# A convolution's sums in a PSUM bank and tile each, its chains in pairs, and another place for sigmoids, scans and gate products

## The chip, the core and the metric

The kernel runs on one core of a Trainium2 chip. The metric is the device time of one execution in microseconds; lower is better. TensorE (PE) multiplies matrices into PSUM, VectorE (DVE) and GpSimd (POOL) work element by element, ScalarE (ACT) does functions such as sigmoid and the casts, SyncE (SP) issues the DMAs. A tile is a piece of on-chip memory with up to 128 partitions; an f32 tile of 128x512 in PSUM is one bank.

## The reference, cut to what matters

One even layer (a Conformer convolution branch and a bidirectional RG-LRU branch beside each other) and one odd layer (a pooling mixer) over 1024 latent tokens and 256 context tokens with 1024 channels. The change lies in the even layer:

```python
z = h @ p["w_in"]
va, vg, ga, xb, gb = split(z)                       # 1024 channels each
u = va * sigmoid(vg)                                # the linear unit
u = depthwise_conv(u, conv_w, conv_b, (15, 15))     # 31 taps along the tokens
y_a = silu(layernorm(u)) * silu(ga)
u2 = depthwise_conv(xb, sconv_w, sconv_b, (2, 1))   # 4 taps, context and latent
r, i = sigmoid(u2 @ w_r + b_r), sigmoid(u2 @ w_i + b_i)    # per head and direction
a = exp(-8 * r * softplus(-lam))
bx = sqrt(1 - a * a) * (i * u2)
h_t = a_t * h_{t-1} + bx_t                          # forwards and backwards
y_b = (h_forward + h_backward) * silu(gb)
out = concatenate([y_a, y_b]) @ w_out
```

## The kernel before

All data lie with channels on the partitions and tokens along the row, so that a channel tile (128 channels) of the 1024 latent tokens is a 128x1024 tile. Each f32 product is made of three matmuls in fp32r: the weights and the activations are split into a high part (a cast on ACT, names `wh_` and `h0h`) and a low part (a subtraction, `wl_` on POOL and `h0l`), and PE adds high x high, high x low and low x high. A product of 128x512 over the 8 tiles of input channels takes 24 matmuls.

The even layer's input projection is a loop over j, the 8 channel tiles (= heads of the LRU). An iteration does, on PE: vg of j (two halves of 512 tokens), va of j, xbc (the context part of xb of j+1, 256 tokens), then the gates of j (12 steps: two directions, two gates, three pieces of tokens) with the product xb of j+1 between them. The other engines follow:
- DVE: the short convolution `uc` of j (a first tap on ACT, three others on DVE: `first_tap`, `other_taps`), `ul` (low part of uc), `u` = va times the sigmoid, the scans of the iteration before (`rec_scan` for each direction: one SCALAR_TENSOR_TENSOR and a scan over the context and one over the latent tokens), their sum (`rec_sum`), and steps of the 31-tap convolution wherever `fill(n)` stands.
- ACT: the cast `uh` of uc, tanh, exp and sqrt of the recurrence of the iteration before (`rec_tanh`, `rec_exp`, `rec_root`), the sigmoids `sg` of vg, those of the gates (named `l`, straight out of PSUM), and casts of weights. A change of the function table costs an ACT_TABLE_LOAD.
- POOL: low parts of weights, `rec_input` (gate times uc) and `rec_scaled` (the same times the root), for each direction.

The 31-tap convolution of a channel tile is a generator, `conv` (L500). It sums even and odd tokens apart: one 128x512 sum `acc_` of the even tokens, one, `late`, of the odd ones, then, after it has added odd and even tokens into `uo`, a second chain of taps with added pairs of weights `wsum`. `fill(n)` takes n steps from the convolution begun first of those whose `u` is whole. The two sums are the two halves of one two-bank tile from `wide` (L91). What stays open when the loop ends is done in pairs of tiles (L910 to L912), outside the written order.

Behind the loop, the products gb of j = 0 to 7 (PE), their silu `sb` (ACT), `yr` = yb_raw times sb (DVE; the sum of the scans comes back from DRAM), its split `ybh`, `ybl`, with conv steps between. Then come the products wob (output projection of y_b), the mean `mu` over `lnsum` (the sum of the finished convolutions, two matmuls on PE), the LayerNorm of u (subtraction, squares, root), and the products ga.

The order of all this is written by hand. The helper `on` (L433, its instruction is issued at L437, which is why the profile shows L437 for nearly all of it) makes an instruction issue behind the last one that `on` gave to the same engine. DMAs go out on SP in the order in which `raw_load` (L463) and the others are called; `raw_split` (L468) casts and subtracts. Where a tile's pool has no free buffer, the instruction that takes one waits for the last reader of the oldest: raw weights `wr`, `wh` and `wl` have 2 buffers each, `t` tiles (sg, sb, split gate weights) 4, one-bank PSUM tiles 4, and of `wide` there is one buffer for each of two tags, `cv` (conv) and `xb`. The six tiles `l` hold gates and roots and are passed on from one iteration to the next.

Of the kernel before, what the change touches and what calls it, by code (L numbers as in the profile page):

```python
# [9 lines left out]
F32 = mybir.dt.float32  # L10
# [45 lines left out]
def body(ctx, tc, xT, ctxT, cc, ccol, modT, modW, win, gw, wout, wu, grp, wg, wo1, small, edge, ident, outT):  # L56
# [34 lines left out]
    def wide(name, n):  # L91
        return pc.tile([P, S], F32, tag=("cv", "xb")[n % 2], name=name)
# [85 lines left out]
    def rstd(acc, eps, name, wn=0):  # L178
        n = acc.shape[-1]
        ps = psum(f"ms_{name}") if n < H else wide(f"ms_{name}", wn)  # L180
        nc.tensor.matmul(ps[:, :n], ones, acc, start=True, stop=True)
        rt = ttile(f"sq_{name}")
        nc.scalar.activation(rt[:, :n], ps[:, :n], AF.Sqrt, bias=eps)
        nc.vector.reciprocal(acc, rt[:, :n])


    def rstd_cols(acc, name, idD, rpool, wn):
        n = acc.shape[-1]
        nt = n // P
        ps = wide(f"ms_{name}", wn)  # L190
# [9 lines left out]
        nc.tensor.matmul(ps[:, H : H + n], ones, t, start=True, stop=True)  # L200
        return ps[:, H : H + n]
# [66 lines left out]
    with ExitStack() as sctx:  # L268
# [99 lines left out]
        for i, t in enumerate((cL, cC)):  # L368
            ps = wide(f"c_{i}", i)
            for h in range(2):  # L370
                nc.tensor.matmul(ps[:, HALF[h]], ones[:1], cx[i][:1, HALF[h]], start=True, stop=True)
            nc.scalar.activation(t, ps, AF.Silu, scale=float(D))
# [127 lines left out]
    def conv(j, n):  # L500
        acp = wide(f"conv{j}", n)
        ue, uo = us[j][:, 0::2], us[j][:, 1::2]
        acc_, late, bias = acp[:, HALF[0]], acp[:, HALF[1]], col(O_CONVB + j)
        w = lambda k: col(O_CONVW + 31 * j + k)
        vec(nc.vector.tensor_scalar, out=acc_, in0=ue, scalar1=w(15), scalar2=None, op0=mult)
# [3 lines left out]
        for n in range(NT + 1):  # L509
# [6 lines left out]
        vec(nc.vector.scalar_tensor_tensor, out=edge_junk, in0=uo[:, H - 8 :], scalar=1.0, in1=taps[:, j, 0:16:2],  # L516
            op0=mult, op1=mult, accum_out=edges[:, j : j + 1])
# [4 lines left out]
        vec(nc.vector.scalar_tensor_tensor, out=acc_, in0=uo, scalar=wsum[:, j, 7:8], in1=ue, op0=mult, op1=sub)  # L522
# [21 lines left out]
    def fill(n):  # L544
        while n > 0:
            try:
# [5 lines left out]
                going[0] = conv(begun[0], 0)  # L552
                begun[0] += 1

    with ExitStack() as actx:
# [79 lines left out]
        xb = wide("xb0", 1)  # L635
# [13 lines left out]
        for j in range(KT):  # L649
# [53 lines left out]
            if state is not None:  # L703
# [6 lines left out]
            xb = wide(name if final else f"xb{j + 1}", 1)  # L710
# [8 lines left out]
            for n, _ in enumerate(gate_steps(j, (gwh, gwl), (uh, ul), gates)):  # L719
# [12 lines left out]
        gps = {0: [xb[:, h] for h in HALF], 1: [psum(f"gb1_{h}") for h in range(2)]}  # L732
# [8 lines left out]
        all_of(mm3_fixed(gps[1][0], w, (hh, hl), HALF[0]))  # L741
# [834 lines left out]
```

## Time and profile before

| what | value |
|---|---|
| runs of the kernel, median of 3 | 1409.15 us (1409.05 to 1413.17) |
| the profiled execution, its own time | 1413.85 us |
| its span | 1412.0 us |
| busy PE / DVE / ACT / POOL | 92% / 86% / 44% / 25% |
| mean granted TensorE clock | 0.962 of full |
| loop over j and its end | 157 to 528 us of the span |
| gb, wob, to the mean of the LayerNorm | 528 to 674 us |
| ga and all behind it | from 718 us |

The profile is of one execution, that of 1413.85 us; times within it count from the start of its span. A row of the timeline has start, length, engine, line, operation, out<-in by the program's names without buffer numbers, matrix or tile sizes and, in brackets, the idle time before it and what ended it; x8 means that eight instructions in a row are shown as one. A row of the waits has the waiting instruction, the one that released it, the total in us, how often, and the longest. A busy share of 92% is a mean over stages with different limits, so the stages have to be looked at one by one.

### The profile page before, as it was taken

How to read it: one execution, taken by the hardware profiler on the slowest of the kernel's cores; microseconds unless marked ns; L12 is line 12 of the kernel's file. 1: busy time of each engine (PE TensorE's matmuls, PEld its weight loads, DVE VectorE, ACT ScalarE, POOL GpSimd, SP SyncE). 2: the span in 40 equal slices, each digit the busy share in tenths (PEclk: the TensorE clock that was granted, in tenths of full speed). 3: DMA queues.
4: the chain of work that ended last, by engine and by line, in shares of the span. 5: the costliest groups of instructions: out<-in, count | busy, mean ns of one | idle time of the engine just before them, and what ended most of it. 6: DMA issues, size and time to landing. Idle time of an engine off the chain costs nothing.

```text
span 1412.0 us, 15817 instructions
## 1 busy us (share of the span) xinstructions
PE 1295.2 (92%) x5664; PEld 1051.2 (74%) x5664; DVE 1215.2 (86%) x1790; ACT 628.3 (44%) x900; POOL 349.0 (25%) x172
## 2 busy tenths in 40 slices
PE   7888999899889839999869999999999999999896
PEld 4467888778777728878658788878878888778685
DVE  7985799999999999989688875899999986976775
ACT  6352745564556522210543534654334433544442
POOL 5182445454544524422402002200000000000002
PEclk9899999999999979999979999999999999999998
DMA  9744011111021212344135436523433334667633
GB/s 352 267 134 157 23 67 38 60 38 68 30 82 38 75 34 93 112 154 152 62 126 185 162 124 203 170 91 134 142 127 113 126 113 142 233 207 249 229 118 120
DMA packets 82866, 181.79 MB, mean 129 GB/s; under 512 B 7778, under 2 KB 27618, under 8 KB 82788
## 3 DMA queue, kind: packets, MB, share of 16 engines
q1 hardware_dynamic: 74340, 176.60, 36.3%
q10 hardware_dynamic: 8448, 4.20, 1.0%
q8 instruction: 44, 0.72, 0.2%
q14 instruction: 34, 0.28, 0.1%
HBM read 136.72 MB, written 44.04 MB: 128 GB/s over the span
## 4 chain that ended last, share of the span: by engine, by line
PE 39%; DVE 26%; DMA 8%; issue 3%; ACT 2%; POOL 2%; POOLq 0%; DVEq 0%; SPq 0%; ACTq 0%
DVE conv L437 7%; DVE l L437 6%; PE gb L437 4%; PE wob L128 2%; PE wob L126 2%; PE wob L127 2%; PE ga L126 2%; PE ga L127 2%; PE ga L128 2%; DVE u L437 2%; DVE uc L437 1%; DMA yr_t<-y_t 1%; DMA wr_wu<-wu 1%; PE qb_g L837 1%; PE qb_g L840 1%
## 5 line engine op out<-in xcount | busy, mean ns | idle before, releaser
L437 DVE SCALAR_TENSOR_TENSOR conv<-u,sm,conv 128x505 f32<-128x505 f32 (+6 forms) x196 | 147.1, 751 | 5.8
L1396 POOL TENSOR_TENSOR o<-x,rr 128x256 f32<-128x256 f32 (+1 forms) x9 | 8.1, 930 | 459.5 <-ACT rr L1384 456.8
L437 ACT ACTIVATE l<-g,sm 128x512 f32<-128x512 f32 (+1 forms) x96 | 58.8, 618 | 83.0 <-PE g L437 60.5
L96 POOL TENSOR_TENSOR wl_wu<-wr_wu,wh_wu 128x1024 fp32r<-128x1024 f32 x16 | 39.4, 2469 | 154.6 <-ACT wh_wu L95 149.5
L437 POOL TENSOR_TENSOR l<-l,uc 128x1280 f32<-128x1280 f32 x16 | 50.3, 3144 | 98.7 <-PE g L437 71.6
L437 PE MATMUL gb<-h0h,wh_gb 128*128 128x512 f32 x128 | 51.7, 404 | 23.0 <-ACT sb L437 23.0
L437 POOL TENSOR_TENSOR l<-l,l 128x1280 f32<-128x1280 f32 x16 | 54.1, 3383 | 72.2 <-ACT l L437 72.2
L437 DVE SCALAR_TENSOR_TENSOR conv<-u,wsum,conv 128x505 f32<-128x505 f32 (+6 forms) x92 | 69.0, 750 | 2.7
L437 DVE TENSOR_TENSOR_SCAN l<-l,l 128x256 f32<-128x256 f32 (+1 forms) x32 | 64.2, 2006 | 1.1
L126 PE MATMUL ga<-h0h,wh_ga 128*128 128x512 f32 x128 | 51.0, 398 | 14.7 <-DVE u L982 14.7
L249 PE MATMUL fold<-gh,wh_wu 128*128 128x512 f32 x128 | 53.1, 416 | 5.3 <-ACT wh_wu L95 5.3
L250 PE MATMUL fold<-gl,wh_wu 128*128 128x512 f32 x128 | 52.3, 408 | 3.2 <-DVE gl L96 3.2
L251 PE MATMUL fold<-gh,wl_wu 128*128 128x512 f32 x128 | 50.6, 404 | 2.3 <-POOL wl_wu L96 2.3
L437 PE MATMUL gb<-h0h,wl_gb 128*128 128x512 f32 x128 | 51.4, 402 | 1.0 <-POOL wl_gb L437 1.0
L437 PE MATMUL gb<-h0l,wh_gb 128*128 128x512 f32 x128 | 51.5, 402 | 0.0
L128 PE MATMUL ga<-h0h,wl_ga 128*128 128x512 f32 x128 | 51.2, 400 | 0.0
L128 PE MATMUL wob<-ybh,wl_wob 128*128 128x512 f32 x128 | 49.7, 393 | 1.3 <-POOL wl_wob L96 1.3
L127 PE MATMUL ga<-h0l,wh_ga 128*128 128x512 f32 x128 | 50.8, 397 | 0.0
L126 PE MATMUL wob<-ybh,wh_wob 128*128 128x512 f32 x128 | 49.7, 393 | 0.5 <-ACT wh_wob L95 0.5
L95 ACT CAST wq_wo<-wr_wo 128x512 fp32r<-128x512 f32 x48 | 28.8, 618 | 47.7 <-DMA wr_wo<-wo 17.7
L437 PE MATMUL vg<-h0l,wh_vg 128*128 128x512 f32 x128 | 49.8, 389 | 0.0
L437 PE MATMUL vg<-h0h,wl_vg 128*128 128x512 f32 x128 | 49.8, 389 | 0.0
(583 smaller groups left out, 4397.6 us busy)
## 6 DMA issues: line engine op xcount, KB each, us to landing
mod<-modT SPq DMA_DIRECT2D x20, 512.0 KB, 6.5
wr_wu<-wu SPq DMA_DIRECT2D x16, 512.0 KB, 3.9
x_part<-xp SPq DMA_DIRECT2D x32, 256.0 KB, 2.4
mod<-modT SPq DMA_DIRECT2D x32, 256.0 KB, 3.3
wr_v<-wfold SPq DMA_DIRECT2D x16, 512.0 KB, 3.8
wr_g<-wg SPq DMA_DIRECT2D x16, 512.0 KB, 4.6
wr_wo<-wo SPq DMA_DIRECT2D x16, 512.0 KB, 4.1
yr_t<-y_t SPq DMA_DIRECT2D x16, 512.0 KB, 6.2
```

What stands on the lines that cost most here:

```text
L95: return (nc.scalar.copy(hi, src), eng.tensor_tensor(out=lo, in0=src, in1=hi.bitcast(F32), op=sub))
L96: eng.tensor_tensor(out=lo, in0=src, in1=hi.bitcast(F32), op=sub))
L126: nc.tensor.matmul(ps, hi[:, kc], xh[k][:, cols], start=(k == 0), stop=False)
L127: nc.tensor.matmul(ps, hi[:, kc], xl[k][:, cols], start=False, stop=False)
L128: nc.tensor.matmul(ps, lo[:, kc], xh[k][:, cols], start=False, stop=(k == ks - 1))
L249: nc.tensor.matmul(ps, wh[:, kc], gh[i], start=(i == 0), stop=False)
L250: nc.tensor.matmul(ps, wh[:, kc], gl[i], start=False, stop=False)
L251: nc.tensor.matmul(ps, wl[:, kc], gh[i], start=False, stop=(i == 3))
L437: last[eng] = f(*args, **kw)
L837: nc.tensor.matmul(ps, hi, xh[k], start=(first and k == 0), stop=False, skip_group_check=not first)
L840: mm = nc.tensor.matmul(ps, lo, xh[k], start=False, stop=(k == KH - 1), skip_group_check=not first)
L1396: nc.gpsimd.tensor_tensor(out=o[:, k - k0], in0=v, in1=rr, op=mult)
```

## The change

Five things are changed.

1. `banks` gives the convolution's two sums a tile and a bank of their own (tags c0 and c1) in place of the halves of one. The other users of `wide` (sums for roots and means) take theirs from it too.
2. `conv`: the second chain of taps alternates between `acc_` and `late`, as the first did. `late` takes the odd tokens' sum (moved by one, with the edge copied into its last column), and the last addition is one instruction of full width. A channel tile has 50 to 52 steps as before. The remaining convolutions behind the loop run one at a time.
3. In an iteration of the loop the sigmoid `sg` of vg's first half stands ahead of the cast `uh`, that of the second half behind it (in the first iteration both ahead). exp, sqrt and the scaled products stand behind the split of the gate weights.
4. Both scans stand behind all taps of xbc. `rec_input` of direction 0 and the split of the next vg's weights are issued at gate step 7 (before: steps 5 and 6). The fills of an iteration are 2, 3 single steps, 2, 9, 6, 4 and 5; before 2, 3 single steps, 4, 8, 5 and 10.
5. gb: products 1 and 2, silu 0 and 1 are issued ahead of the last scans; in the loop over gb the silu of j, the weights and the product of j+2 come ahead of `yr` of j-1.

```diff
-    def wide(name, n):
-        return pc.tile([P, S], F32, tag=("cv", "xb")[n % 2], name=name)
+    def wide(name):
+        return pc.tile([P, S], F32, tag="xb", name=name)
+    def banks(name, n):
+        if n % 2:
+            t = wide(name)
+            return [t[:, h] for h in HALF]
+        return [pc.tile([P, H], F32, tag=f"c{i}", name=f"{name}_{i}") for i in range(2)]
...
-    def conv(j, n):
-        acp = wide(f"conv{j}", n)
+    def conv(j):
+        acc_, late = banks(f"conv{j}", 0)
...
-        for n in range(NT + 1):
-            if n != 7:
-                tap(acc_, uo, wsum[:, j, n : n + 1] if n < NT else w(30), n - 7, n == NT)
-                yield
-        vec(nc.vector.scalar_tensor_tensor, out=uo[:, : H - 1], in0=uo[:, : H - 1], scalar=bias, in1=late[:, 1:],
-            op0=add, op1=sub)
-        vec(nc.vector.scalar_tensor_tensor, out=uo[:, H - 1 :], in0=uo[:, H - 1 :], scalar=bias,
-            in1=edges[:, j : j + 1], op0=add, op1=sub)
+        vec(nc.vector.scalar_tensor_tensor, out=late[:, : H - 1], in0=uo[:, 1:], scalar=both(8), in1=late[:, 1:],
+            op0=mult, op1=sub)
+        vec(nc.vector.tensor_copy, out=late[:, H - 1 :], in_=edge_)
+        yield
+        for i, n in enumerate([n for n in range(NT) if n not in (7, 8)]):
+            tap((acc_, late)[i % 2], uo, both(n), n - 7)
+            yield
+        tap(acc_, uo, both(NT), NT - 7, True)
+        yield
+        vec(nc.vector.scalar_tensor_tensor, out=uo, in0=uo, scalar=bias, in1=late, op0=add, op1=add)
...
-            if state is not None:
-                rec_exp(state)
+            sg = [ttile(f"sg{j}_{h}") for h in range(2)]
+            act(sg[0], vg[0], AF.Sigmoid)
+            all_of(mm3_fixed(vg[1], w, (hh, hl), HALF[1]))
+            if state is None:
+                act(sg[1], vg[1], AF.Sigmoid)
...
             cast(uh, uc)
-            all_of(mm3_fixed(vg[1], w, (hh, hl), HALF[1]))
-            fill(4)
+            if state is not None:
+                act(sg[1], vg[1], AF.Sigmoid)
+            fill(2)
...
-                rec_root(state)
-                rec_scaled(state, 0)
...
-                rec_scaled(state, 1)
-            sg = []
-            for h in range(2):
-                sg.append(ttile(f"sg{j}_{h}"))
-                act(sg[h], vg[h], AF.Sigmoid)
+                rec_exp(state)
+                rec_root(state)
+                for d in range(2):
+                    rec_scaled(state, d)
...
-                fill((8, 5)[h])
+                fill((9, 6)[h])
...
-            if state is not None:
-                rec_scan(state, 0)
+            fill(4)
             if not final:
                 other_taps(j + 1, xc, ucn[:, :C])
             if state is not None:
-                rec_scan(state, 1)
+                for d in range(2):
+                    rec_scan(state, d)
                 rec_sum(state)
...
-                if n == 5:
+                if n == 7:
+                    w = raw_split(raw, name)
                     rec_input(now, 0)
-                if n == 6:
-                    w = raw_split(raw, name)
             all_of(steps)
-            fill(10)
+            fill(5)
...
+        gb_product(2, gws[2])
...
+        gb_silu(0)
+        gb_silu(1)
+        fill(24)
...
-    for j in range(KT):
...
+    for j in range(1, KT + 1):
+        if 1 < j < KT:
+            gb_silu(j)
+        gb_weights(j + 2)
         if j + 2 < KT:
...
+            gb_product(j + 2, gws[j + 2])
+        n = j - 1
...
-        gb_weights(j + 3)
...
-    for j in range(begun[0], KT, 2):
-        all_of(zip(*[conv(k, n) for n, k in enumerate(range(j, min(j + 2, KT)))]))
+    for j in range(begun[0], KT):
+        all_of(conv(j))
```

First, DVE in the loop, where the convolution of a channel tile begins and the taps of `uc` follow. `conv_0` and `conv_1` are the two sums of the kernel after; the bracket names the engines that an instruction waits for, and DVE there means an instruction ahead on DVE itself. Before:

```order
L437 TENSOR_SCALAR conv_2225<-u_1667,sm 128x512
L437 TENSOR_SCALAR conv_2225<-u_1667,sm 128x512 [waits DVE_49]
L437 SCALAR_TENSOR_TENSOR conv_2225<-u_1667,sm,conv_2225 128x505 [waits DVE_49]
L437 SCALAR_TENSOR_TENSOR conv_2225<-u_1667,sm,conv_2225 128x504 [waits DVE_49]
L437 SCALAR_TENSOR_TENSOR conv_2225<-u_1667,sm,conv_2225 128x506 [waits DVE_49]
L437 SCALAR_TENSOR_TENSOR conv_2225<-u_1667,sm,conv_2225 128x505 [waits DVE_49]
L437 SCALAR_TENSOR_TENSOR uc_2090<-xb_2103,sm,uc_2090 128x1022 [waits Activation_49]
L437 SCALAR_TENSOR_TENSOR conv_2225<-u_1667,sm,conv_2225 128x507 [waits DVE_49]
```

After:

```order
L445 TENSOR_SCALAR conv_0_2258<-u_1666,sm 128x512
L445 TENSOR_SCALAR conv_1_2259<-u_1666,sm 128x512
L445 SCALAR_TENSOR_TENSOR uc_2094<-xb_2111,sm,uc_2094 128x1022 [waits Activation_49]
L445 SCALAR_TENSOR_TENSOR conv_0_2258<-u_1666,sm,conv_0_2258 128x505 [waits DVE_49]
L445 SCALAR_TENSOR_TENSOR uc_2094<-xb_2111,sm,uc_2094 128x1023 [waits DVE_49]
L445 SCALAR_TENSOR_TENSOR conv_1_2259<-u_1666,sm,conv_1_2259 128x504
L445 SCALAR_TENSOR_TENSOR uc_2094<-xb_2111,sm,uc_2094 128x1023 [waits DVE_49]
L445 SCALAR_TENSOR_TENSOR conv_0_2258<-u_1666,sm,conv_0_2258 128x506
```

Before, both sums are in `conv_2225`, and each instruction waits for the one ahead of it. After, `conv_0` and `conv_1` take turns: the second of each pair waits for nothing on DVE, or for the one before the one ahead.

Second, ACT in one iteration, from the cast of va's weights to the first tap on the next context part (`l` are the tiles of the recurrence; `cneg` marks exp, `tiny` sqrt). Before:

```order
L437 CAST wh_va_1937<-wr_va_1935 128x1024 [waits DMAHW3_49]
L437 ACT_TABLE_LOAD
L437 ACTIVATE l_828<-l_828,cneg 128x1280 [waits Activation_49]
L437 ACTIVATE l_829<-l_829,cneg 128x1280 [waits Activation_49]
L437 CAST uh_1943<-uc_1760 128x1280 [waits DVE_49]
L437 ACT_TABLE_LOAD
L437 ACTIVATE l_827<-l_827,tiny 128x1280
L437 ACTIVATE l_830<-l_830,tiny 128x1280
L437 CAST wh_xb_1982<-wr_xb_1980 128x1024 [waits DMAHW5_49,PE_49,Pool_49]
L437 CAST wh_gw_1986<-wr_gw_1988 128x512 [waits DMAHW6_49]
L437 ACT_TABLE_LOAD
L437 ACTIVATE sg_0_1993<-vg_0_1897 128x512
```

After:

```order
L445 CAST wh_va_1940<-wr_va_1938 128x1024 [waits DMAHW3_49]
L445 ACTIVATE sg_0_1944<-vg_0_1900 128x512 [waits PE_49]
L445 CAST uh_1971<-uc_1764 128x1280 [waits DVE_49,Activation_49]
L445 ACTIVATE sg_1_1945<-vg_1_1901 128x512 [waits PE_49]
L445 CAST wh_xb_1980<-wr_xb_1978 128x1024 [waits DMAHW5_49,Pool_49]
L445 CAST wh_gw_1984<-wr_gw_1986 128x512 [waits DMAHW6_49]
L445 ACT_TABLE_LOAD
L445 ACTIVATE l_832<-l_832,cneg 128x1280 [waits Activation_49]
L445 ACTIVATE l_833<-l_833,cneg 128x1280 [waits Activation_49]
L445 ACT_TABLE_LOAD
L445 ACTIVATE l_831<-l_831,tiny 128x1280
L445 ACTIVATE l_834<-l_834,tiny 128x1280
```

The sigmoids `sg` stood behind the casts of all weights and now stand on both sides of `uh`; exp and sqrt with their table loads moved behind `wh_gw`.

Third, POOL in one iteration (`l<-l,uc` is `rec_input`, `l<-l,l` is `rec_scaled`, `wl_` are low parts of weights). Before:

```order
L437 TENSOR_TENSOR l_830<-l_830,uc_1760 128x1280 [waits DVE_49,DMAHW4_49,Activation_49,Pool_49]
L437 TENSOR_TENSOR wl_vg_2168<-wr_vg_2063,wh_vg_2167 128x1024 [waits DMAHW7_49,PE_49,Activation_49]
L437 TENSOR_TENSOR l_829<-l_829,uc_1760 128x1280 [waits DVE_49,Activation_49]
L437 TENSOR_TENSOR wl_va_2271<-wr_va_2268,wh_va_2270 128x1024 [waits DMAHW0_49,PE_49,Activation_49]
L437 TENSOR_TENSOR l_830<-l_830,l_825 128x1280 [waits Activation_49,Pool_49]
L437 TENSOR_TENSOR wl_xb_2314<-wr_xb_2311,wh_xb_2313 128x1024 [waits DMAHW2_49,PE_49,Activation_49]
L437 TENSOR_TENSOR wl_gw_2318<-wr_gw_2319,wh_gw_2317 128x512 [waits DMAHW3_49,Activation_49]
L437 TENSOR_TENSOR l_829<-l_829,l_826 128x1280 [waits DVE_49,Pool_49]
```

After:

```order
L445 TENSOR_TENSOR wl_vg_2183<-wr_vg_2067,wh_vg_2182 128x1024 [waits PE_49,DMAHW7_49,Activation_49,Pool_49]
L445 TENSOR_TENSOR l_834<-l_834,uc_1764 128x1280 [waits DMAHW4_49,DVE_49,Pool_49]
L445 TENSOR_TENSOR l_833<-l_833,uc_1764 128x1280 [waits DVE_49,Activation_49]
L445 TENSOR_TENSOR wl_va_2274<-wr_va_2271,wh_va_2273 128x1024 [waits DMAHW0_49,PE_49,Activation_49]
L445 TENSOR_TENSOR wl_xb_2314<-wr_xb_2311,wh_xb_2313 128x1024 [waits DMAHW2_49,PE_49,Activation_49]
L445 TENSOR_TENSOR wl_gw_2318<-wr_gw_2319,wh_gw_2317 128x512 [waits DMAHW3_49,Activation_49]
L445 TENSOR_TENSOR l_834<-l_834,l_829 128x1280 [waits Activation_49,Pool_49]
L445 TENSOR_TENSOR l_833<-l_833,l_830 128x1280 [waits DVE_49,Activation_49,Pool_49]
```

The split of vg's weights now stands ahead of both `rec_input`, and both scaled products stand behind the splits of xb and gw.

More of the change, by code (lines that the diff above doesn't have):

```diff
@@ L179, in rstd @@
         n = acc.shape[-1]
-        ps = psum(f"ms_{name}") if n < H else wide(f"ms_{name}", wn)
+        ps = psum(f"ms_{name}") if n < H else banks(f"ms_{name}", wn)[0]
         nc.tensor.matmul(ps[:, :n], ones, acc, start=True, stop=True)
@@ L189, in rstd_cols @@
         nt = n // P
-        ps = wide(f"ms_{name}", wn)
+        ps, root = banks(f"ms_{name}", wn)
         r = rpool.tile([P, H // P], F32, tag="rc", name=f"rc_{name}")[:, :nt]
@@ L368, in body @@
         for i, t in enumerate((cL, cC)):
-            ps = wide(f"c_{i}", i)
+            ps = banks(f"c_{i}", i)
             for h in range(2):
-                nc.tensor.matmul(ps[:, HALF[h]], ones[:1], cx[i][:1, HALF[h]], start=True, stop=True)
-            nc.scalar.activation(t, ps, AF.Silu, scale=float(D))
+                nc.tensor.matmul(ps[h], ones[:1], cx[i][:1, HALF[h]], start=True, stop=True)
+            for h in range(2):
+                nc.scalar.activation(t[:, HALF[h]], ps[h], AF.Silu, scale=float(D))
         def ctx_load(i):
@@ L521, in conv @@
         yield
-        vec(nc.vector.scalar_tensor_tensor, out=acc_, in0=uo, scalar=wsum[:, j, 7:8], in1=ue, op0=mult, op1=sub)
+        vec(nc.vector.scalar_tensor_tensor, out=acc_, in0=uo, scalar=both(7), in1=ue, op0=mult, op1=sub)
         yield
@@ L739, in gb_weights, with gb_product, gb_silu @@
                 gws[j] = raw_split(raw_load(wout[j - KT, 1], f"wob{j - KT}"), f"wob{j - KT}")
-        all_of(mm3_fixed(gps[1][0], w, (hh, hl), HALF[0]))
+        def gb_product(j, w):
+            gps[j] = [psum(f"gb{j}_{h}") for h in range(2)]
+            for h in range(2):
+                all_of(mm3_fixed(gps[j][h], w, (hh, hl), HALF[h]))
+        sbs = {}
+        def gb_silu(j):
+            sbs[j] = [ttile(f"sb{j}_{h}") for h in range(2)]
+            for h in range(2):
+                act(sbs[j][h], gps[j][h], AF.Silu)
+        gb_product(1, w)
         rec_input(state, 1)
@@ L750, in body @@
             rec_scaled(state, d)
-        sbs = {0: [ttile(f"sb0_{h}") for h in range(2)]}
-        for h in range(2):
-            act(sbs[0][h], gps[0][h], AF.Silu)
-        fill(20)
+        gb_silu(0)
+        gb_silu(1)
+        fill(24)
         for d in range(2):
@@ L1438, in body @@
     nc.scalar.activation(dsh[:, 0:1], fin[0][:, 0:1], AF.Sqrt)
-    fps = [wide(f"fin_ms{h}", h) for h in range(2)]
+    fps = [banks(f"fin_ms{h}", h) for h in range(2)]
     first, second = slice(H, H + H // 2), slice(H + H // 2, S)
```

44 lines of the change are left out of this document (18 added, 26 removed).

## The prediction

> **What bounds the kernel now.** I read the busy time by stage first, then the waits, then the timeline of PE and of DVE. The page alone says PE 92% and DVE 86%, which is an average over stages; the stages tell which of the two ends last. Columns: stretch, its length, busy time of PE, PEld, DVE, ACT, POOL with instruction counts, granted clock, DMA share, GB/s.
>
> ```profile
> core 0: us, PE busy (x) PEld busy (x) DVE busy (x) ACT busy (x) POOL busy (x), PEclk, DMA share, GB/s
> 157.70:200.20 42.50, 42.50 (x206) 35.86 (x205) 40.20 (x41) 26.24 (x30) 22.83 (x9) 1.00 0.14 46
> 244.10:293.60 49.50, 45.63 (x205) 38.38 (x204) 48.23 (x55) 27.73 (x32) 23.57 (x9) 0.93 0.14 48
> 505.00:528.00 23.00, 0.00 (x0) 0.00 (x0) 22.40 (x27) 3.24 (x6) 2.68 (x3) 0.58 0.13 46
> 587.00:678.00 91.00, 89.29 (x389) 72.60 (x388) 77.37 (x117) 13.28 (x17) 23.86 (x12) 1.00 0.41 143
> ```
>
> The first row is iteration j=1 of the channel-tile loop: PE has no idle time, so one iteration costs PE 42.5 us. The second is an iteration two later with the same matmuls: 49.5 us, DVE busy for 48.2 of it. From 505 to 528 PE does nothing while DVE is full. So DVE sets the time of the loop and of its end, and only in 587 to 678 is PE the bound (89.3 of 91).
>
> ```profile
> ACT uh L437 <- DVE uc L437: 29.4, 6, 5.5
> PE xbc L437 <- ACT sg L437: 13.2, 4, 5.6
> PE gb L437 <- ACT sb L437: 23.0, 1, 23.0
> ACT ybh L437 <- DVE yr L437: 74.3, 15, 20.9
> 157.68 0.39 PE L437 MATMUL vg<-h0h,wh_vg 128*128 128x512 f32 x1
> 435.04 0.39 PE L437 MATMUL vg<-h0h,wh_vg 128*128 128x512 f32 x1
> 159.13 1.28 DVE L437 SCALAR_TENSOR_TENSOR uc<-xb,sm,uc 128x1022 f32<-128x1022 f32 x1 [7.64 <-ACT uc L437]
> 447.09 1.27 DVE L437 SCALAR_TENSOR_TENSOR uc<-xb,sm,uc 128x1022 f32<-128x1022 f32 x1
> ```
>
> The waits (total, times, longest) name the path: DVE is late with the taps of uc, so ACT's cast uh is late, so the sigmoids sg behind it are late, and PE stands before xbc because a PSUM bank is not free. The one wait of 23.0 us is the same thing at the end: silu sb stands on ACT behind a cast ybh that waits for DVE's yr. PE's six iterations from 157.68 to 435.04 took 277.4 us, against 6 x 42.5 = 255.0. DVE's first tap of uc stood 1.45 us behind PE's start at j=1 and 12.05 behind at j=7: DVE needs (447.09 - 159.13)/6 = **48.0 us** per iteration.
>
> **What is in DVE's 48.0.** First the convolution.
>
> ```profile
> 303.11 0.74 DVE L437 SCALAR_TENSOR_TENSOR conv<-u,sm,conv 128x507 f32<-128x507 f32 x1
> 303.76 1.27 DVE L437 SCALAR_TENSOR_TENSOR uc<-xb,sm,uc 128x1023 f32<-128x1023 f32 x1
> 304.96 0.74 DVE L437 SCALAR_TENSOR_TENSOR conv<-u,sm,conv 128x506 f32<-128x506 f32 x1
> 312.00 6.28 DVE L437 SCALAR_TENSOR_TENSOR conv<-u,sm,conv 128x509 f32<-128x509 f32 x8
> L437 DVE SCALAR_TENSOR_TENSOR conv<-u,sm,conv 128x505 f32<-128x505 f32 (+6 forms) x196 | 147.1, 751 | 5.8
> ```
>
> Eight taps in a row start 6.28/8 = 0.785 us apart; in the program order each waits for the one ahead. Where a tap of uc stands between two of conv, the instruction behind starts 0.65 us after a tap of 0.74 (303.11 to 303.76), and 1.20 after one of 1.27: without a wait for the one ahead, an instruction starts 0.08 before that one ends, with it 0.04 behind. A wait removed is therefore worth 0.785 - 0.65 = **0.13 us** (0.127 unrounded). Then the collisions with GpSimd:
>
> ```profile
> 277.86 3.08 DVE L437 TENSOR_TENSOR_SCAN l<-l,l 128x256 f32<-128x256 f32 x2
> 283.78 5.68 DVE L437 TENSOR_TENSOR_SCAN l<-l,l 128x256 f32<-128x256 f32 x2
> 289.50 3.25 DVE L437 TENSOR_TENSOR l<-l,l 128x1024 f32<-128x1024 f32 x1
> 517.82 1.23 DVE L437 TENSOR_TENSOR l<-l,l 128x1024 f32<-128x1024 f32 x1
> 284.36 2.96 POOL L437 TENSOR_TENSOR l<-l,uc 128x1280 f32<-128x1280 f32 x1 [9.87 <-PE g L437]
> 287.26 4.41 POOL L437 TENSOR_TENSOR wl_vg<-wr_vg,wh_vg 128x1024 fp32r<-128x1024 f32 x1
> ```
>
> The scans of direction 0 take 3.08 us, those of direction 1 5.68 and the sum 3.25 instead of 1.23, while POOL runs rec_input and wl_vg at 284 to 292: 2.6 + 2.0 = 4.6 us lost here. The undisturbed durations of an iteration's 50 DVE instructions add up to 42.5, so 48.0 holds 5.5 of this on the mean. The 196 taps of conv have a mean of 0.751 against 0.74 alone: they, with an operand in PSUM, are not stretched.
>
> **The change, part by part.** (1) *Conv.* Of the 50 DVE instructions of an iteration 33 wait for the one ahead before, and some 15 of 49 after; one conv step moves out. That is 18 x 0.127 + 0.75 = 3.05: 42.5 becomes **39.4**. No row shows two instructions in a row that both write PSUM without a wait: their gain lies between 0 and 0.13 (a loss has no row: the mixed pairs all gain); I take 0.127, the nearest row, and keep 0 as a rival. The copied edge and the full-width last add swap two instructions for two, at nothing. Beyond the loop the waits removed are 34 between j=7's tap and the first yr, 51 between first and last yr, 36 from there to the first mu, with 3, 1 and 3 instructions more of 0.65 in them (those that left the stages before). Their undisturbed sums are 67.3, 78.2 and 62.0 us before, so 67.3 - 4.3 + 2.0 = **65.0**, 78.2 - 6.5 + 0.65 = **72.4**, 62.0 - 4.6 + 2.0 = **59.4** after.
>
> (2) *Scans and rec_input.* rec_input(0) and wl_vg now run in the last gates; the scans follow the taps of xbc at 26 to 37 us of an iteration. By the order POOL has by then wl_va, wl_xb, wl_gw and the two scaled products; walked through with their durations it ends near 26 us and has nothing until wl_vg near 37. What collides is left at 0.5 to 3 us; I take 1.3, so DVE needs 40.7, less than PE's 42.5. Bounds: 0, and the 5.5 of before.
>
> (3) *Sigmoids.* sg0 ahead of uh no longer waits for DVE, so a bank comes free some 5 us earlier; sg1 still stands behind uh, and uh behind the taps. The cover is DVE's being on time. exp and sqrt move behind the casts of weights: two table loads as before, and the scans that need them stand behind all the taps. They and POOL's scaled products are moved past the splits of wl_xb and wl_gw in POOL's queue and past the loads of these in SP's: what that costs if a load is late is the slower rival.
>
> (4) *gb.* Products 1 and 2 run ahead of the last scans, silu 0 and 1 too; PE's 23.0 us hole then has work of 24 to 48 matmuls and no silu behind a cast ybh. Nothing is added but order; fill(24) for fill(20) is conv work that stands elsewhere before.
>
> **The sum**, along DVE to the LayerNorm.
>
> ```profile
> 518.96 0.69 DVE L437 TENSOR_TENSOR yr<-yr,sb 128x512 f32<-128x512 f32 x1
> 600.79 0.68 DVE L437 TENSOR_TENSOR yr<-yr,sb 128x512 f32<-128x512 f32 x1
> 601.50 0.62 ACT L437 CAST ybh<-yr 128x512 fp32r<-128x512 f32 x1 [4.93 <-DVE yr L437]
> 602.20 1.29 POOL L437 TENSOR_TENSOR ybl<-yr,ybh 128x512 fp32r<-128x512 f32 x1 [4.23 <-ACT ybh L437]
> 611.75 0.49 PE L128 MATMUL wob<-ybh,wl_wob 128*128 128x512 f32 x1 [1.25 <-POOL wl_wob L96]
> 668.12 0.39 PE L126 MATMUL wob<-ybh,wh_wob 128*128 128x512 f32 x1
> 673.78 0.39 PE L127 MATMUL wob<-ybl,wh_wob 128*128 128x512 f32 x1
> 674.01 1.02 PE L917 MATMUL mu<-lnsum,ones 128*128 128x512 f32 x2
> 675.07 1.28 DVE L920 TENSOR_TENSOR u<-u,mu 128x512 f32<-128x512 f32 x2 [3.28 <-PE mu L917]
> 718.18 0.80 PE ga L126
> ```
>
> First tap of j=7: 157.7 + 255.0 + 1.45 = 414 (447 before). Before, the next two stages took 71.9 and 81.8, that is 4.6 and 3.6 above their undisturbed sums; I keep 3 in each. First yr: 414 + 65.0 + 3 = 482 (519). Last yr: 482 + 72.4 + 3 = 557 (600.8). Its cast and split (0.62 + 1.29), the last products that need them and the start of the third wob (1.25 of waiting for its low half) put that at 562.3. From there 263 matmuls stand ahead of mu, at 0.227 (25 starts between 668.12 and 673.78): 59.7, so mu at **622** (674.0). DVE gets there at 557 + 59.4 + 3 to 6 = 619 to 622: level. That is 52 us earlier. Behind it the LayerNorm holds PE until 718.18, 43.1 us after DVE's first subtraction, with the same DVE and ACT instructions and the same order after, so I carry the 52 to the end. The profiled execution took 1413.85 us (span 1412.0); 1413.85 - 52 = 1361.9. The runs' median, 1409.15, is 4.7 lower than that execution, so the forecast is **1357**.
>
> **Rivals.** *Conv without waits gains nothing* (the 0 above). DVE is then 42.5 less one step plus 1.3 of collisions, 43.3 per iteration: j=7 at 419, first yr at 493, last at 578, mu near 650, 24 us earlier: 1385. For it: no row of two such instructions in a row. Against: the mixed pairs at 303 to 305 gain on both sides. The Trainium skill has this as a rule: "VectorE: DVE Perf Modes", section "The DRAIN you can't avoid", says that eight copies took 13.88 us with a semaphore after each and the same with one after the last, so that only fewer instructions help. By it the time would be this rival's; the 0.65 beside 0.785 in this trace disagrees, and so I give it little. Chance 0.08.
>
> *Collisions stay.* With 5.5 per iteration DVE needs 44.9, 2.4 more than PE, 14 us more at j=7, and half of that again is lost behind: mu near 640, 34 us earlier: 1375. For it: POOL's work is as long as before, and a late POOL meets the scans again. Chance 0.15.
>
> *No loss at all.* PE alone from 157.7: 255.0, then 863 wide matmuls and 12 narrow to mu, 197: 609.7, 64 us earlier: 1345. Chance 0.07.
>
> *Slower: scans wait for POOL.* The scaled products now queue behind wl_xb and wl_gw.
>
> ```profile
> wr_gw<-gw SPq DMA_DIRECT2D x8, 256.0 KB, 2.6
> L437 POOL TENSOR_TENSOR l<-l,l 128x1280 f32<-128x1280 f32 x16 | 54.1, 3383 | 72.2 <-ACT l L437 72.2
> ```
>
> If the load of gw is late, its split and both products (3.38 each) are, DVE stands at the scans and the gates' sigmoids that overwrite the scanned tiles hold PE. It eats the gain when 52/7 = 7.4 us are lost per iteration, beyond some 2 of slack: the second product would end at 35 to 36 rather than 26. Against: the load lands 2.6 us after its issue, and its place in the queue is the same. Ending at 40 it loses 14 - 2 = 12 per iteration: 1357 + 7 x 12 = 1441. Chance 0.03. That the order comes out other than written, no change: 0.01.
>
> **Numbers.** Forecast 0.66, its own range 1350 to 1366 (collisions 0.5 to 3 per iteration, twice the slip after the loop). The others 0.08, 0.15, 0.07, 0.03, 0.01. The range 1345 to 1377 takes in the fastest rival and the collisions, and leaves out the first rival, the slower case and the tails. A measurement of this kernel can tell some 0.3%, 4.2 us, from no change; faster by more 0.96, within 0.01, slower 0.03.
>
> **What would show it.** Taps of conv in pairs 0.65 apart (right) or 0.785; PE's loop iterations at 42.5 with no wait of xbc for sg; scans near 0.69 and 2.35 each with POOL idle; no 23 us hole in gb; mu at 622 and the LayerNorm's 43 unchanged. It is wrong if PE waits in the gates for sigmoids that wait for scans, or if a second hole opens at the casts ybh.

## The result, and the profile after

| | before | after | ratio (95% interval) |
|---|---|---|---|
| median of the runs | 1410.13 us (4 runs, 1409.05 to 1413.17) | 1394.55 us (4 runs, 1390.64 to 1395.02) | 0.988 (0.9856 to 0.9904) |
| profiled execution, its span | 1413.85, 1412.0 | 1395.02, 1393.2 | |

The change makes the kernel 15.6 us faster. The forecast was 1357, in a range of 1345 to 1377: less than a third of the gain came. In the profiles the step from 1413.85 to 1395.02 is 18.8 us. All places below are of these two profiles unless a run is named.

The same stages as before, with the columns as there (length, busy time of PE, PEld, DVE, ACT, POOL with counts, granted clock, DMA share, GB/s): two iterations of the loop, the hole at gb, and the stretch up to the mean of the LayerNorm.

```profile
199.20:243.60 44.40, 43.29 (x205) 35.57 (x204) 44.05 (x50) 27.41 (x32) 23.95 (x9) 1.00 0.16 54
330.60:380.30 49.70, 44.74 (x205) 37.28 (x204) 49.07 (x55) 26.25 (x30) 23.66 (x9) 0.93 0.15 52
502.00:514.00 12.00, 0.17 (x1) 0.00 (x0) 11.83 (x16) 3.43 (x6) 2.55 (x2) 0.71 0.23 88
587.00:652.00 65.00, 64.33 (x267) 51.99 (x267) 56.66 (x86) 7.18 (x7) 16.97 (x7) 0.93 0.49 166
```

DVE is still full in the loop (44.05 of 44.4, 49.07 of 49.7) and PE still is not. The hole at gb has shrunk from 23 to 12 us, and now the last stage has a granted clock of 0.93, where it was 1.00.

The waits of the kernel after (total, times, longest):

```profile
ACT uh L445 <- DVE uc L445: 25.4, 7, 7.9
PE gb L445 <- ACT wh_gb L445: 12.1, 1, 12.1
ACT ybh L445 <- DVE yr L445: 70.1, 15, 18.0
PE ga L133 <- DVE u L1001: 13.5, 1, 13.5
```

PE's wait of xbc for the sigmoids (13.2 us in four waits) is gone, as the new place of `sg` wanted. But the cast `uh` still waits for DVE's taps, for 25.4 us where it was 29.4, and PE now waits in the gates for DVE's `u` instead (9.3 us in six waits; 0.3 before). Here is where DVE and PE stand: first and last iteration's start on PE, first tap of `uc` at j=1 and j=7, first and last `yr`, and `mu`.

```profile
156.28 0.39 PE L445 MATMUL vg<-h0h,wh_vg 128*128 128x512 f32 x1
423.86 0.39 PE L445 MATMUL vg<-h0h,wh_vg 128*128 128x512 f32 x1
157.72 1.28 DVE L445 SCALAR_TENSOR_TENSOR uc<-xb,sm,uc 128x1022 f32<-128x1022 f32 x1 [12.41 <-ACT uc L445]
432.03 1.27 DVE L445 SCALAR_TENSOR_TENSOR uc<-xb,sm,uc 128x1022 f32<-128x1022 f32 x1
505.34 0.68 DVE L445 TENSOR_TENSOR yr<-yr,sb 128x512 f32<-128x512 f32 x1
583.32 0.69 DVE L445 TENSOR_TENSOR yr<-yr,sb 128x512 f32<-128x512 f32 x1
651.96 0.59 PE L936 MATMUL mu<-lnsum,ones 128*128 128x512 f32 x1
```

DVE needs (432.03 - 157.72)/6 = 45.7 us per iteration: 48.0 before, 40.7 in the forecast. Is it the convolution that did not get cheaper, or the collisions that did not go? Nine taps in a row answer the first question:

```profile
302.79 5.97 DVE L445 SCALAR_TENSOR_TENSOR conv<-u,sm,conv 128x506 f32<-128x506 f32 x9
L445 DVE SCALAR_TENSOR_TENSOR conv<-u,sm,conv 128x505 f32<-128x505 f32 (+6 forms) x196 | 134.1, 742 | 0.8
```

They start (5.97 - 0.74)/8 = 0.654 us apart, where it was 0.785. The pairs gain all that the forecast took. So DVE's time has to be split. For each DVE instruction I take the shortest instance of the same operation, operands and shape in the traces of all runs as its undisturbed length; what an instance has above that (where it is more than 0.25 us) is called stretch, gaps in which DVE is idle are taken out, and the rest is the undisturbed sum.

| stage | before: sum + stretch | forecast: sum + stretch | after: sum + stretch |
|---|---|---|---|
| per iteration, j=1 to 7 | 42.5 + 5.5 | 39.4 + 1.3 | 39.3 + 6.3 |
| j=7's tap to the first yr | 67.3 + 4.6 | 65.0 + 3 | 64.6 + 8.7 |
| first to last yr | 78.0 + 3.8 | 72.4 + 3 | 71.6 + 6.4 |

(Some expectations below give the stretch before as 5.2; by this count it is 5.5.) The sums are within 0.8 us of the forecast. The stretch did not fall, it rose. Which instructions are stretched, and by what? The kernel after, DVE first, then POOL, at the end of an iteration and at the start of gb:

```profile
324.00 3.08 DVE L445 TENSOR_TENSOR_SCAN l<-l,l 128x256 f32<-128x256 f32 x2
327.12 3.24 DVE L445 TENSOR_TENSOR l<-l,l 128x1024 f32<-128x1024 f32 x1
333.35 3.34 DVE L445 TENSOR_TENSOR u<-u 128x512 f32<-128x512 f32 x1
515.04 2.23 DVE L445 TENSOR_TENSOR yr<-yr,sb 128x512 f32<-128x512 f32 x1
325.36 3.92 POOL L445 TENSOR_TENSOR wl_vg<-wr_vg,wh_vg 128x1024 fp32r<-128x1024 f32 x1 [9.92 <-DVE l L445]
329.24 6.90 POOL L445 TENSOR_TENSOR l<-l,uc 128x1280 f32<-128x1280 f32 x2
336.32 2.63 POOL L445 TENSOR_TENSOR wl_va<-wr_va,wh_va 128x1024 fp32r<-128x1024 f32 x1 [0.18 <-ACT wh_va L445]
514.37 2.35 POOL L445 TENSOR_TENSOR wl_gb<-wr_gb,wh_gb 128x1024 fp32r<-128x1024 f32 x1 [0.70 <-ACT wh_gb L445]
```

In this iteration the scans are free (3.08, as alone). But the sum of the scans (1.23 alone) takes 3.24 beside vg's split; `u<-u` (uo = uo + ue inside `conv`, 0.69 alone) takes 3.34 beside `rec_input`; yr (0.68) takes 2.23 beside gb's split. The last pair is the clearest: yr starts 0.67 us into wl_gb, wl_gb ends at 514.37 + 2.35 = 516.72, and yr ends at 517.27, 0.55 behind it. So yr did not run slowly: it stood until GpSimd's instruction was over and then ran. And wl_vg, that starts in a scan, is the one that is long (3.92 against 2.4). That reads like a lock that is held for a whole instruction, and the experiments test it. The other instructions agree: from j=1's first tap to the last yr 30 DVE instructions of this kernel are stretched, each has two inputs in SBUF, and each ends by its own length, less 0.12 to 0.20 us, behind the end of a GpSimd instruction that was running when it started.

How the delay begins is seen at j=1, DVE first, then POOL:

```profile
176.94 2.20 DVE L445 SCALAR_TENSOR_TENSOR edge_junk<-u,sm 128x8 f32<-128x8 f32 x1
179.18 3.39 DVE L445 TENSOR_TENSOR u<-u 128x512 f32<-128x512 f32 x1
193.94 5.03 DVE L445 TENSOR_TENSOR_SCAN l<-l,l 128x256 f32<-128x256 f32 x2
199.00 3.79 DVE L445 TENSOR_TENSOR l<-l,l 128x1024 f32<-128x1024 f32 x1
207.30 1.26 DVE L445 SCALAR_TENSOR_TENSOR uc<-xb,sm,uc 128x1022 f32<-128x1022 f32 x1
176.16 5.86 POOL L445 TENSOR_TENSOR l<-l,l 128x1280 f32<-128x1280 f32 x2 [3.52 <-ACT l L445]
194.37 2.45 POOL L445 TENSOR_TENSOR wl_vg<-wr_vg,wh_vg 128x1024 fp32r<-128x1024 f32 x1 [12.35 <-DVE l L445]
196.78 8.85 POOL L445 TENSOR_TENSOR l<-l,uc 128x1280 f32<-128x1280 f32 x2
```

Beside the scaled products the convolution's edge (`edge_junk`, 0.15 alone) and `u<-u` lose 4.8 us; so late, the second pair of scans (3.08 alone) meets vg's split and the sum meets `rec_input`, 4.5 us more. The scans are caught like this in three of the six iterations, the sum in all six.

The Trainium skill states it: "SBUF — State Buffer", section "Who interferes with whom", says that VectorE and GpSimd share one pair of SBUF ports under an exclusive lock, that a VectorE instruction with two SBUF inputs contends for it with a GpSimd instruction that reads SBUF, and that one with at most one SBUF input, outside the engine's two-port modes, does not. The trace agrees: 2.23 for the yr above, and 0.742 on the mean for 196 taps whose second operand is in PSUM.

### The profile page after: what moved, and what is told of

Its sections match the earlier page's. It is cut to its first block, busy times and chain, and to the rows that moved or that the text cites. A ratio compares the mean times of both kernels' runs of the same rounds, so it can differ in the third digit from the quotient of the medians.

```text
span 1393.2 us, 15819 instructions
## 1 busy us (share of the span) xinstructions
PE 1293.3 (93%) x5664; PEld 1046.3 (75%) x5664; DVE 1204.9 (86%) x1790; ACT 627.7 (45%) x902; POOL 353.0 (25%) x172
## 5 line engine op out<-in xcount | busy, mean ns | idle before, releaser
L445 DVE SCALAR_TENSOR_TENSOR conv<-u,sm,conv 128x505 f32<-128x505 f32 (+6 forms) x196 | 134.1, 742 | 0.8
L133 PE MATMUL ga<-h0h,wh_ga 128*128 128x512 f32 x128 | 50.9, 398 | 13.5 <-DVE u L1001 13.5
L445 PE MATMUL gb<-h0h,wh_gb 128*128 128x512 f32 x128 | 51.0, 399 | 12.1 <-ACT wh_gb L445 12.1
L445 POOL TENSOR_TENSOR l<-l,uc 128x1280 f32<-128x1280 f32 x16 | 61.9, 3891 | 0.0
L445 DVE SCALAR_TENSOR_TENSOR conv<-u,wsum,conv 128x506 f32<-128x506 f32 (+3 forms) x88 | 60.2, 743 | 0.2
L445 DVE TENSOR_TENSOR_SCAN l<-l,l 128x256 f32<-128x256 f32 (+1 forms) x32 | 56.5, 1767 | 1.1
L445 POOL TENSOR_TENSOR l<-l,l 128x1280 f32<-128x1280 f32 x16 | 47.8, 3010 | 27.0 <-ACT l L445 22.8
L134 PE MATMUL wob<-ybl,wh_wob 128*128 128x512 f32 x128 | 51.8, 404 | 0.6 <-POOL ybl L445 0.6
L445 PE MATMUL va<-h0h,wl_va 128*128 128x512 f32 x128 | 50.0, 391 | 0.0
L445 PE MATMUL va<-h0l,wh_va 128*128 128x512 f32 x128 | 49.8, 389 | 0.0
```

The lines of the kernel that those rows point to most:

```text
L133: nc.tensor.matmul(ps, hi[:, kc], xh[k][:, cols], start=(k == 0), stop=False)
L134: nc.tensor.matmul(ps, hi[:, kc], xl[k][:, cols], start=False, stop=False)
L445: last[eng] = f(*args, **kw)
```

## The experiments

Chips differ by some us (the kernel before has medians of 1410 to 1417 us), so ratios are to the kernel before on the same chip. "Stretch" and "sum" are per iteration from j=1 to j=7, split as above; what an iteration has beyond the two is idle time of DVE (0.5 to 0.8 us in e5, e7, e8, e10 and e12, 1.5 in e11, at most 0.1 in the others).

| run | median us | ratio (95%) | sum + stretch | j=7's tap |
|---|---|---|---|---|
| changed kernel | 1394.55 | 0.988 (0.9856 to 0.9904) | 39.3 + 6.3 | 432.0 |
| e1_conv | 1388.72 | 0.9816 (0.9788 to 0.9844) | 40.1 + 6.1 | 434.9 |
| e2_order | 1414.07 | 0.9998 (0.998 to 1.0017) | 41.4 + 5.9 | 441.0 |
| e3_gate5 | 1396.52 | 0.9874 (0.9845 to 0.9903) | 39.3 + 7.0 | 435.5 |
| e5_sum_pool | 1369.96 | 0.9688 (0.9661 to 0.9716) | 38.1 + 4.7 | 418.4 |
| e6_input64 | 1379.94 | 0.9756 (0.9733 to 0.978) | 39.3 + 4.3 | 420.9 |
| e7_sum_pool_gb0 | 1369.29 | 0.9681 (0.9655 to 0.9708) | 38.1 + 4.9 | 420.1 |
| e8_conv_sum_pool | 1366.01 | 0.966 (0.9638 to 0.9683) | 38.8 + 4.5 | 422.9 |
| e9_gb0 | 1391.48 | 0.9836 (0.9811 to 0.9861) | 39.3 + 6.2 | 432.0 |
| e10_half | 1369.25 | 0.968 (0.9629 to 0.9731) | 39.5 + 2.9 | 415.0 |
| e11_quarter | 1361.69 | 0.9628 (0.959 to 0.9665) | 39.7 + 1.3 | 409.2 |
| e12_e8_quarter | 1360.43 | 0.9623 (0.9584 to 0.9663) | 39.0 + 3.2 | 414.8 |
| e13_before_quarter | 1389.13 | 0.9808 (0.9782 to 0.9833) | 42.5 + 2.6 | 428.1 |

**The parts apart: e1_conv and e2_order.** e1_conv has `banks` and the new `conv` (parts 1 and 2 of the change) and the loop and gb of before; e2_order has parts 3 to 5 and this in place of the new convolution:

```diff
-        acc_, late = banks(f"conv{j}", 0)
+        acp = wide(f"conv{j}", n)
+        acc_, late = acp[:, HALF[0]], acp[:, HALF[1]]
...
+            if n != 7:
+                tap(acc_, uo, wsum[:, j, n : n + 1] if n < NT else w(30), n - 7, n == NT)
```

> Only the convolution is changed (a bank and tile for each sum, all chains in pairs); loop and gb are ordered as before. Theory A, contention: DVE's time is its undisturbed sum plus what GpSimd stretches; the sum falls from 42.5 to 39.4 us per iteration and the stretch stays near the 5.2 of before, so DVE's first tap of uc at j=7 lies near 430 (447 before), the hole of PE at gb stays but ends some 22 us earlier, 1386 to 1391 us. Rival B: a faster DVE meets more of GpSimd's work whatever the order; stretch 6 or more per iteration, 1391 to 1398. Rival C: the order alone made the gain; 1406 to 1413.

> Only the order is changed (sigmoids, scans, gb); the convolution has its two sums in one two-bank tile and the second chain single, as before. Theory A: undisturbed sum 42.5 per iteration, stretch some 6.3 as in the changed kernel, so DVE needs 48 to 49; the hole at gb is smaller all the same: 1403 to 1420 us. Rival C, the order made the gain: 1392 to 1398. If the order really takes the collisions away once DVE is slow (stretch under 2): 1390 to 1395, with 44 us per iteration.

The convolution alone gives 1.8%, more than the whole change, and the two intervals do not overlap. The order alone gives nothing that can be measured. So all of the gain is the convolution's, and the new order takes some of it back. e1_conv came out as theory A had it in time (1388.72), though its stretch of 6.1 is rival B's (6 or more) rather than that of before, and its j=7 tap lies at 434.9 rather than 430. Its own wait at gb:

```profile
PE gb L445 <- ACT sb L445: 21.0, 1, 21.0
```

It still has nearly the whole hole of before and is faster all the same: the hole as such was not what cost the time.

**The places: e3_gate5 and e9_gb0.** e3_gate5 puts `rec_input` of direction 0 back at gate step 5 and vg's split at 6; e9_gb0 has the gb part (`gps` to the end of the loop over gb) of before in the changed kernel.

```diff
-                if n == 7:
-                    w = raw_split(raw, name)
-                    rec_input(now, 0)
+                if n == 5:
+                    rec_input(now, 0)
+                if n == 6:
+                    w = raw_split(raw, name)
```

> The changed kernel with rec_input of direction 0 back at gate step 5 and vg's split at 6. Theory A: GpSimd's 7 us of work start some 3 us earlier and meet the scans of direction 1 and the sum; stretch 5 to 8 per iteration, 1390 to 1402 us. Rival: the place at step 7 does what it says and takes half of the collisions away; back at 5 and 6 the stretch is 8 or more and the time 1402 to 1410.

> The changed kernel with the gb part alone in the order of before. If the gb part is what makes the changed kernel slower than e1_conv, 1384 to 1389 us; if it is the order in the loop, 1393 to 1400.

e3_gate5 is the changed kernel's time within the intervals, with a stretch of 7.0 in place of 6.3: GpSimd's work met the scans and the SCALAR_TENSOR_TENSOR in front of them (4.7 to 4.8 us in each of the six iterations), and the sum in none. Moving it by three us only chose other victims. e9_gb0 lies between its two expectations and its interval meets those of both neighbours: which of the two, gb's order or the loop's, costs what against e1_conv stays open.

**Fewer collisions: e5_sum_pool and e6_input64.** e5_sum_pool gives the sum of the scans to GpSimd, behind vg's split (the last one of all stays on DVE):

```diff
-                rec_sum(state)
             xb = wide(name if final else f"xb{j + 1}")
...
                 if n == 7:
                     w = raw_split(raw, name)
+                    if state is not None:
+                        rec_sum(state)
                     rec_input(now, 0)
```

e6_input64 cuts GpSimd's work instead: `rec_input` multiplies 64 of its 1280 columns and leaves the rest out.

```diff
-            gp(out=iu, in0=iu, in1=st[1], op=mult)
+            gp(out=iu[:, :64], in0=iu[:, :64], in1=st[1][:, :64], op=mult)
```

> The changed kernel with the sum of both scans (rec_sum) on GpSimd behind vg's split, but for the last. Theory A: DVE loses its 1.22 us and the 2.0 to 3.3 by which it is stretched; 41 to 43 us per iteration, so PE sets the loop; 1372 to 1382 us. Rival D: the longer work on GpSimd meets other instructions of DVE and the stretch per iteration stays at 6 or more: 1384 to 1390. Rival E: the scans hold GpSimd's queue, so rec_input comes late for the scaled products and ACT: 1394 or more.

> The changed kernel with rec_input on 64 of its 1280 columns only (the rest of the product is left out), so some 7 us per iteration go from GpSimd and nothing from DVE. Theory A, contention: the stretch of DVE falls from 6.3 per iteration to 2 or 3 (what vg's split does to the sum), the first tap of uc at j=7 moves from 432 to 412 to 418, 1368 to 1378 us. Rival: DVE's long instructions are long for a reason of its own, or other work on GpSimd takes the place; stretch 5 or more, 1388 to 1396.

One instruction of 1.23 us per iteration, given from DVE to GpSimd, is worth 1.9% (0.9688 against 0.988): j=7's tap comes 13.6 us earlier over six iterations, 2.3 each, 1.2 of it the instruction itself and 1.6 less stretch, of which 0.5 us is lost again as idle time of DVE. The time is a little below theory A's range, though DVE needs 43.5 us per iteration and not 41 to 43. e6 takes nothing from DVE, and still j=7's tap comes 11 us earlier: work on GpSimd alone lengthens DVE's. The size was smaller than expected: 4.3 of stretch are left rather than 2 to 3, and 1379.94 us lies just above theory A's range. vg's split still cost 2.0 us in every iteration, on the last scan in four and on the sum in two, and `u<-u` was still stretched in three.

**The order again, with fewer collisions: e7 and e8.** e7_sum_pool_gb0 is e5 with the gb part of before, e8_conv_sum_pool is e1_conv with the sum on GpSimd, by the same edits.

> The sum on GpSimd as in e5_sum_pool, but the gb part in the order of before. If PE, once it resumes, has work enough to the LayerNorm (129 us without a gap in e1_conv), its longer hole is free and the gaps before wob go: the mean of the LayerNorm at 620 to 625 (630 in e5), 1360 to 1367 us. Rival: the shorter hole is worth what it is shorter by; 1374 to 1382.

> e1_conv (only the convolution changed) with the sum of both scans on GpSimd. Theory A: 40.5 less 1.2 undisturbed, the stretch falls from 5.7 by some 2, so 42.5 to 43.5 us per iteration without any of the new order; mean of the LayerNorm at 621 to 628; 1362 to 1372. Rival: without the new place of the scans the sum on GpSimd comes late for tanh and the gates; 1376 or more.

e7 met neither expectation: `mu` at 631.6 is no earlier than e5's 630.3, and the time is the same. e8 is as fast as e5 and e7 without any of the new order (0.966, the three intervals overlap).

**The lock itself: e10 to e13.** If a DVE instruction stands until GpSimd's is over, shorter instructions on GpSimd must help though the bytes and the work stay. If both share a bandwidth they must not.

```diff
-    def gp(*args, **kw):
-        return on("pool", nc.gpsimd.tensor_tensor, *args, **kw)
+    def gp(out, in0, in1, op):
+        n = out.shape[-1] // 4 if out.shape[-1] > H else out.shape[-1]
+        for a in range(0, out.shape[-1], n):
+            on("pool", nc.gpsimd.tensor_tensor, out=out[:, a : a + n], in0=in0[:, a : a + n], in1=in1[:, a : a + n], op=op)
```

(e10_half has 2 for 4; e13 is the kernel before with this edit alone.)

> The changed kernel with every GpSimd instruction of more than 512 columns in two halves. Theory A2, a lock: an instruction of DVE with both operands in SBUF that starts while GpSimd works waits for the end of GpSimd's instruction (yr at 515.04 ends 0.55 behind wl_gb's end at 516.72 in the changed kernel). Then half as long an instruction holds it half as long: stretch 6.3 per iteration to 3 to 4, 1378 to 1386 us. Rival F, both share a bandwidth: the same bytes, the same stretch (6 or more), and GpSimd's work is longer by a start per piece: 1393 to 1399.

> The same in quarters (256 or 320 columns). Theory A2, a lock: stretch 1.5 to 2.5 per iteration, so DVE needs 41 to 42 us and PE sets the loop: first tap of uc at j=7 before 418, 1364 to 1376 us. Rival F, bandwidth: 1393 to 1400. Rival G: GpSimd gets in between DVE's instructions only with a wait of its own, so its work comes late for the scans: 1390 or more.

> e8_conv_sum_pool (convolution changed, sum on GpSimd, order as before) with GpSimd's instructions in quarters. Theory A2: the stretch of 4.2 per iteration falls to 1 to 2; DVE is then ahead of PE in the loop, so only the rest of the gain shows: 1352 to 1361 us. Rival F: 1364 to 1372.

> The kernel before, unchanged but for GpSimd's instructions of more than 512 columns in quarters. Theory A2, the lock: its stretch of 5.2 per iteration falls to 1.5 to 2.5, its undisturbed sum stays 42.5, so DVE needs 44 to 45 us: first tap of uc at j=7 near 427 (447), the 23 us hole at gb stays; 1385 to 1394 us. That is the lock's share alone; what e12 and e11 have beyond it is the convolution's. Rival: the quarters gain as much without the convolution (1368 or less), so the pairs would be worth nothing once the lock is short.

The times of bandwidth sharing (rival F) did not come. In the changed kernel the stretch goes 6.3, 2.9, 1.3 with halves and quarters, and the time 0.988, 0.968, 0.9628, in e10 and e11 a little better than theory A2's ranges. And in all fourteen profiles each stretched DVE instruction between j=1's first tap and the last yr, 391 in all, ends as above: its own length, less some 0.1 to 0.2 us, behind the end of a GpSimd instruction. That is what shows the lock. With halves the stretch falls by more than half: a DVE that is on time also meets fewer. In e11_quarter, DVE and then GpSimd, at the end of the iteration that was shown above:

```profile
316.24 1.23 DVE L445 TENSOR_TENSOR l<-l,l 128x1024 f32<-128x1024 f32 x1
321.18 1.31 DVE L445 TENSOR_TENSOR u<-u 128x512 f32<-128x512 f32 x1
317.45 2.83 POOL L445 TENSOR_TENSOR wl_vg<-wr_vg,wh_vg 128x256 fp32r<-128x256 f32 x4 [10.64 <-issue]
320.23 3.83 POOL L445 TENSOR_TENSOR l<-l,uc 128x320 f32<-128x320 f32 x4
```

The sum is on time and meets nothing; `u<-u`, that starts in the middle of rec_input's quarters, loses 0.6 us where it lost 2.7. The rest of e11's profile, an iteration by engine, PE's start at j=1 and j=7, and the same marks as above:

```profile
152.70:195.20 42.50, 42.50 (x205) 35.85 (x205) 39.75 (x50) 26.37 (x30) 24.03 (x29) 1.00 0.15 49
152.75 0.39 PE L445 MATMUL vg<-h0h,wh_vg 128*128 128x512 f32 x1
407.63 0.39 PE L445 MATMUL vg<-h0h,wh_vg 128*128 128x512 f32 x1
409.23 1.27 DVE L445 SCALAR_TENSOR_TENSOR uc<-xb,sm,uc 128x1022 f32<-128x1022 f32 x1
478.38 0.68 DVE L445 TENSOR_TENSOR yr<-yr,sb 128x512 f32<-128x512 f32 x1
555.04 0.68 DVE L445 TENSOR_TENSOR yr<-yr,sb 128x512 f32<-128x512 f32 x1
620.41 0.59 PE L938 MATMUL mu<-lnsum,ones 128*128 128x512 f32 x1
```

PE runs six iterations in 407.63 - 152.75 = 254.9 us, 42.5 each, which leaves no room for a gap: it is the bound of the loop at last. e12 (order as before) is as fast as e11, in 0.9623 with a wide overlap, though it has 3.2 us of stretch left where 1 to 2 were expected: its meetings are shorter, but 43 DVE instructions are stretched where e8 has 23. Against e8 (0.966) its gain is not clear of the noise. In e13 DVE stays the bound at 45.1 per iteration. Its 0.9808 and e1_conv's 0.9816 multiply to 0.9627, near what e11 and e12 measure, as if the pairs and the shorter hold of the lock were two gains that add up. That is not shown: no run has these two alone (e11 has the new order as well, e12 the sum on GpSimd). e11 and e12 are the fastest of all runs.

## Why the prediction was wrong, point by point

- *What bounds the kernel* (DVE in the loop and at its end) was right: DVE is idle for under 1 us from 157.7 to the last yr, before and after.
- *Conv, 0.127 us for each wait that goes, 42.5 to 39.4* was right: 0.654 between starts and 39.3. The value between 0 and 0.13 that no row showed is 0.13. The rival "conv without waits gains nothing" is out (its sum is also 0.25 us too high: 42.5 - 0.75 + 1.3 is 43.05 per iteration, not 43.3). With it goes, for this instruction, the rule that it took from the Trainium skill, "VectorE: DVE Perf Modes", section "The DRAIN you can't avoid": the same tap costs 0.785 with a wait for the one ahead and 0.654 without. The same section also says that a next instruction that is not held starts earlier, and with that the trace agrees.
- *"What collides is left at 0.5 to 3 us; I take 1.3, so DVE needs 40.7, less than PE's 42.5"* is the step that failed, and with it the 3 us that I kept in each of the two later stages. The runs show 6.3, 8.7 and 6.4. Two things were wrong in it. I looked at the scans and the sum only and called the convolution safe because its taps have an operand in PSUM; but `u<-u`, the first tap of the second chain, the edge and `lnsum` have both in SBUF and take up to 2.7 us more each, 3.0 of the 6.3. And I laid GpSimd's work beside a DVE that keeps pace with PE. At j=1 the scaled products ran where I had them (176.2 to 182.0, 20 to 26 us into the iteration) and vg's split too (38 us; I had 37), but DVE, held by the first, was not yet through its scans and sum when the second began. 9.3 us of stretch in this one iteration put its next first tap 8.1 us behind PE (207.3 against 199.2), and so on from there: the scans and the sum have the other 3.3 of the 6.3. Behind the first yr the 6.4 lie on six of the yr, each beside a split of weights.
- *The sum* therefore slipped by 18 us at j=7's tap (432.0 for 414), 23 at the first yr, 26 at the last (583.3 for 557) and 30 at mu (652.0 for 622). The last 4 go with the clock: between 587 and 652 the granted clock is 0.93, and 267 matmuls take 64.3 us, 0.241 each, where the forecast had 0.227 from a stretch at 1.00; that is 3.7 us.
- *The LayerNorm's 43.1 us and all behind it* held: 44.6 us from mu to ga's restart (651.96 to 696.58, the wait of 13.5 us of ga for u), 44.2 before. From there to the end it took 696.6 us, against 693.8 before; where these 3 us come from is open.
- *Where the collisions do go, the forecast's numbers come out.* e11_quarter has the 1.3 us of stretch that I assumed. Its marks are 409.2, 478.4, 555.0 and 620.4 (forecast 414, 482, 557 and 622), and its profiled execution took 1360.7 us, where I had 1361.9. Some of that closeness is luck: its j=1 tap comes 3.5 us earlier than the changed kernel's (154.2 against 157.7), and its two later stages have 3.1 and 1.1 us of stretch, where I kept 3 in each, with 1.2 and 3.1 us of idle time of DVE besides.
- *The rival "collisions stay"* was what happened. Its time, 1375, was too early: it had 5.5 in the loop and little behind, and the stretch rose in all three stages. (By its own terms, 14 us and half of that again, it should have said 1378.)
- *gb.* The hole went from 23.0 to 12.1 as the new order wanted, but the cast wh_gb that ends it stands on ACT behind the casts of the first two yr, and PE then waits 2.9 us for the last yr's halves (2.3 for ybh, 0.6 for ybl), for which it did not wait before. Undoing it (e9, e7) costs nothing that can be measured.

## What to carry to other kernels

Before an order is tuned, list on DVE every instruction with both inputs in SBUF and on GpSimd every instruction that reads SBUF: one that meets the other waits for its end, so the loss is the rest of the holder's length, and it shifts everything behind. Moving work by a few us only picks the next victim; what helped in the old order and in the new is to cut the holder into pieces; quarters made a split of 2.40 us on GpSimd 0.4 us longer and both kernels faster (e13, e11). And lay such work beside the late engine's real position, not beside the pace it should have.

## What the runs showed of the hardware that was not expected

Two taps in a row that both write PSUM, each in a bank of its own, overlap as well as one in PSUM with one in SBUF: 0.654 us from start to start, 0.08 before the first one ends, against 0.65 in the mixed pairs of before. Before, each sum filled a bank as well; what differs is the wait for the instruction ahead. vg's split took 2.83 us in four pieces in e11_quarter, beside a busy DVE, and 2.40 whole in e5_sum_pool (321.32), so cutting it cost 0.4 us there. The lock works both ways: vg's split took 3.92 us in the changed kernel where it had to stand behind a scan.
